# A hybrid decoder layer on one core: start addresses of split weights, and transposes in four visits instead of eight

## The chip, the cores and the metric

The kernel runs on one core of a Trainium2 chip. The metric is the device time of one execution in microseconds (us); below stands the median of several runs. One more execution was taken with the hardware profiler: the trace and the profile's page come from it.

## The reference

One layer over 256 tokens of 2048 features (batch 1), all in float32: two token mixers side by side (an mLSTM in chunks and an RWKV-7 scan), a cross-attention into 256 memory tokens, and a feed-forward part with a causal convolution and a GELU gate. Each part stands between two RMS norms and is added to the residual stream. Cut to what matters:

```python
h = rms_norm(x, mix_pre_norm)
proj = h @ w_in                                  # 2048 x 10536
ha = mlstm_chunkwise(q, k, v, i, f) ...          # 4 heads, chunks of 64 tokens
hb = rwkv7_scan(r, decay, k, v, kk, kk * a) ...  # 16 heads of 64
merged = sigmoid(g_a) * (ha @ w_branch_a) + sigmoid(g_b) * (hb @ w_branch_b)
x = x + rms_norm(merged @ w_mix_out, mix_post_norm)
x = x + rms_norm(cross_attention(rms_norm(x), rms_norm(mem), wq, wkv, wo), xattn_post_norm)
u = rms_norm(x, ffn_pre_norm) @ w_up             # 2048 x 16384
uc = conv_b + sum(conv_w[j] * shift_right(u, 2 - j) for j in range(3))
gate, up = split_cols(uc, (8192, 8192))
x = x + rms_norm((gelu(gate) * up) @ w_down, ffn_post_norm)
```

## The kernel before

**Products in split form.** A float32 product is made of three matmuls in the chip's faster 32-bit format (fp32r): each operand is split into a high part, rounded to that format, and the low rest. For activations these are pairs such as `hh`, `hl` or `fh`, `fl`; for weights `wh`, `wl`. A product is high x high, low x high and high x low. The file's helper `mm` records every matmul on line 181.

**Weight chunks.** All weights come in 648 chunks of 128 partitions x 1024 elements or fewer (512 KB), numbered 0 to 647 in the order of use. A transfer on SyncE's queue loads each into `raw`, ACT casts it to `wh` (line 401), VectorE subtracts to make `wl` (line 441), and TensorE uses both. Transfers run six chunks ahead, casts and subtractions up to three. `wh` and `wl` have four buffers each, taken in turn, so chunks with the same number modulo 4 share one.

**Two forms.** In an "fm" block (features on partitions) 128-column pieces of the weights are the stationary operand, loaded into the array by LDWEIGHTS, and 256 tokens of activations stream past as the moving operand. A chunk has two halves (k = 2 rows of 512 columns) and 24 matmuls. In a "tm" block (tokens on partitions) the activations are stationary and the weights move: 512 columns a matmul, or 296 in the small projection (`w_sm`, chunks 8 to 15, 12 matmuls a chunk). The block "xv" moves 256 columns.

**Order.** Chunks 0 to 7 are RWKV's first projection, 8 to 15 the small one, 16 to 103 the other RWKV and mLSTM projections, 104 to 199 the gates and branches, 200 to 231 the mixer's output, 232 to 263 the cross-attention (xk 232 to 239, xv 240, 241 and 250 to 255, xq 242 to 249, xo 256 to 263), 264 to 519 the up-projection (blocks fu0 and fu1 interleaved, then fu2 at 280 to 287, fu3 at 288 and so on) and 520 to 647 the down-projection (fd0, fd1).

**Side work.** Evacuation of blocks, norms, the scan and attention are generators that `Spread` runs a piece at a time between half chunks: `half()` advances a tick, so a chunk has two ticks. A generator added with `chain=n` has one piece every n ticks, the first after `phase` ticks. Pieces that need TensorE put their matmuls into the stream at that place. `x_tokens` is such a generator: it is started in the evacuation of fu0, transposes the residual stream (`xr`, features by tokens) into `xt` (tokens by features) through PSUM tiles `xt` of the pool `aux` (four banks), and ACT copies each tile out. `xt` is used at the very end of the kernel. The block fu2 holds two `aux` banks until its evacuation.

**Where a chunk lies in its buffer.** `staged` gives each `wh` and `wl` a view into a buffer of 1152 elements: it starts at element `o`, and its second half lies `e` elements behind the first. Usually `o` is 16 (64 bytes), and 0 for "tm" chunks of 512 columns and more. A chunk in the table `KICK` is shifted: kind 2 starts it 96 bytes in instead of 64, so that both halves are shifted; kind 0 does so too and puts the second half another 96 bytes on; kind 1 shifts only the second half, by 32 bytes.

Of the kernel before, what the change touches and what calls it, by code (L numbers as in the profile page):

```python
# [15 lines left out]
P = 128  # L16
# [123 lines left out]
def layer(tc, d, dbg=None):  # L140
    with ExitStack() as ctx:
        ctx.enter_context(tc.manual_schedule())
        _layer(ctx, tc, tc.nc, d, dbg or (lambda n, t: None))


def _layer(ctx, tc, nc, d, dbg):
    act, dve = Meter(nc.scalar, 200.0, 0.83), Meter(nc.vector, 70.0, 1.04)
    pool, pe, sp = nc.gpsimd, nc.tensor, nc.sync
    side = Spread(act, dve)
# [6 lines left out]
    def U(name, shape=None, dt=F32):  # L156
        return mp.tile(shape or [P, 8, S], dt, tag="U", bufs=7, name=name)
# [10 lines left out]
    def C(name, tag, shape=None, dt=F32):  # L168
        return mp.tile(shape or [P, S], dt, tag=tag, bufs=1, name=name)
# [7 lines left out]
    def aux(name, shape=None):  # L177
        return pp.tile(shape or [P, 512], F32, tag="aux", bufs=4, name=name)
# [63 lines left out]
    def bc(ap, n):  # L242
        return ap.unsqueeze(1).broadcast_to((ap.shape[0], n, ap.shape[1]))
# [94 lines left out]
    def block(kind, srcs, xs, evac, before=None, cols=512, pool_=None, pre=None, bankwise=False, tail=0):  # L338
# [2 lines left out]
                           pool=pool_ or acc, pre=pre, task=None, bankwise=bankwise, tail=tail))  # L341
        return blocks[-1]

    KICK = {16: 0, 18: 2, 36: 2, 52: 1, 60: 2, 104: 0, 108: 0, 111: 0, 116: 0, 117: 1, 120: 1, 134: 0, 138: 2, 140: 0, 159: 1,
            168: 0, 216: 2, 219: 2, 236: 2, 243: 2, 257: 2, 266: 2}

    HB = [slice(0, 256), slice(256, 512)]

    class Feed:
# [34 lines left out]
        def staged(self, name, r, i):  # L384


            k, c = r.shape[1:]
            kick = KICK.get(i)
            e = -(-c // 64) * 64
            o = 0 if c >= 512 and self.kind[i] == "tm" else 16  # L390
            if kick is not None:
                o, e = ((24, e + 24), (o, e + 8), (24, e))[kick]
            w = wp.tile([P, 1024 + 128], F32R, tag=name, bufs=4, name=name)
            return w[:, o:o + k * e].rearrange("p (k c) -> p k c", k=k)[:, :, 0:c]
# [1447 lines left out]
    def actile(k):  # L1842
        while len(M["ac"]) <= (k // 16 if k < 32 else 2 + (k - 32) // 8):
            n = len(M["ac"])
            M["ac"].append(big("ac") if n < 2 else U("ac"))
        return M["ac"][k // 16][:, k % 16] if k < 32 else M["ac"][2 + (k - 32) // 8][:, (k - 32) % 8]

    def fu_evac(b):
        def gen(ps):
            us = [C("us", f"bg{g}", [P, 2, S]) for g in range(2)]  # L1850
            tt = [[C("tg", f"m{j}") for j in range(2)], [C("tu", f"mt{j}") for j in range(2)]]
            cv = M["cv"]

            def base(i):
                for j in range(2):
                    f = i * 64 + b * 2 + j
                    act.activation(tt[i][j], us[i][:, j], AF.Identity, scale=cv[:, 2, f:f + 1], bias=cv[:, 3, f:f + 1])

            def taps(i):
                for j in range(2):  # L1860
                    f = i * 64 + b * 2 + j
                    o, u = tt[i][j], us[i][:, j]
                    dve.scalar_tensor_tensor(o[:, 1:S], u[:, 0:S - 1], cv[:, 1, f:f + 1], o[:, 1:S],
                                             op0=ALU.mult, op1=ALU.add)
                    dve.scalar_tensor_tensor(o[:, 2:S], u[:, 0:S - 2], cv[:, 0, f:f + 1], o[:, 2:S],
                                             op0=ALU.mult, op1=ALU.add)

            if b == 0:
                yield from M["res"].wait(30)
                side.add(x_tokens(), chain=8)  # L1870
            dve.tensor_mul(us[0], ps[0], bc(stf.rb, 2))
            yield
            base(0)
            dve.tensor_mul(us[1], ps[1], bc(stf.rb, 2))
            yield
            base(1)
            taps(0)
            yield
            for j in range(2):
                act.activation(tt[0][j], tt[0][j], AF.Gelu_apprx_tanh)  # L1880
            taps(1)
            yield
            for j in range(2):
                dve.tensor_mul(actile(b * 2 + j), tt[0][j], tt[1][j])
            yield
        return gen
# [49 lines left out]
    def x_tokens():  # L1936

        M["xt"] = []
        for f in range(4):
            if f % 2 == 0:  # L1940
                M["xt"].append(U("xt", [P, 2, 1024]))
            for t in range(2):
                q = aux("xt", [P, 4, P])
                for j in range(4):
                    k = f * 4 + j
                    pe.transpose(q[:, j], M["xr"][k // 8][:, k % 8, t * P:(t + 1) * P], ident)  # L1946
                act.copy(M["xt"][f // 2][:, t, f % 2 * 512:f % 2 * 512 + 512], q.rearrange("p a b -> p (a b)"))
                yield

    def load_gain():  # L1950
        M["gain"] = mp.tile([P, D], F32, tag="hT", bufs=2, name="gain")
# [175 lines left out]
```

## Time and profile before

| | us |
|---|---|
| median of 3 runs (1863.1 to 1864.75) | 1863.75 |
| the profiled execution's own time | 1862.86 |
| its span, first to last instruction | 1861.0 |
| TensorE busy | 1851.9 |
| VectorE busy | 1296.2 |
| ScalarE (ACT) busy | 1015.3 |
| transposes `xt`, first and last start | 856.8 and 936.5 |

The profiled execution is 1.86 us longer than its span; what lies around the span is the start and the end of the program. "PE" in the rows is TensorE's matmuls, "PEld" its weight loads, "DVE" is VectorE. Matmuls overlap in the array, so the length of a row is more than its share of the time: what counts is the distance from one start to the next. In rows of the time-ordered view the first number is the start in us from the span's start, the second the length, and xN the number of instructions merged into the row.

### The profile page before, as it was taken

The numbers are of one execution on the slowest core, as the hardware profiler recorded it, in microseconds if no ns is written. First come the engines' busy times: TensorE is split into PE (matmuls) and PEld (weight loads), VectorE is DVE, ScalarE is ACT, GpSimd is POOL, SyncE is SP. The second block draws the span as 40 slices with busy tenths as digits, with TensorE's granted clock in tenths as the row PEclk, the third lists the DMA queues.
The fourth block names the chain that finished last, engine by engine and source line by source line (L and its number), as shares of the span: only waits on it lengthen the run. The fifth ranks groups of instructions, "written<-read, shape, count | busy, mean of one in ns | idle before, by whom it ended". The sixth has DMA issues, their size and how long they took to land.

```text
span 1861.0 us, 36212 instructions
## 1 busy us (share of the span) xinstructions
PE 1851.9 (100%) x14930; PEld 1767.3 (95%) x14930; DVE 1296.2 (70%) x1834; ACT 1015.3 (55%) x1493; POOL 34.8 (2%) x64
## 2 busy tenths in 40 slices
PE   9999999999999999999999999999999999999998
PEld 9999888999999999999999999999999988888887
DVE  7889787566676858787766667766666775556555
ACT  6776445555454746666554455444445554545544
POOL 0100020000000000000000000000000000000000
PEclk9999999999999999999999999999999999999999
DMA  7556545455556765555666666666666666666664
GB/s 263 192 174 192 181 153 163 133 164 156 177 190 195 273 203 182 161 183 172 197 196 195 196 193 193 192 193 195 195 196 194 195 193 215 192 193 192 194 192 145
DMA packets 98486, 351.47 MB, mean 189 GB/s; under 512 B 10960, under 2 KB 11984, under 8 KB 97936
## 3 DMA queue, kind: packets, MB, share of 16 engines
q1 hardware_dynamic: 97744, 348.23, 59.8%
q8 instruction: 117, 1.92, 0.4%
q10 hardware_dynamic: 576, 0.92, 0.1%
q14 instruction: 49, 0.40, 0.1%
HBM read 347.01 MB, written 2.10 MB: 188 GB/s over the span
## 4 chain that ended last, share of the span: by engine, by line
PE 99%; DMA 0%; DVE 0%; ACT 0%; issue 0%; DVEq 0%; ACTq 0%
PE fm L181 69%; PE tm L181 25%; DMA w<-in_w_in_dram 0%; PE gram L181 0%; PE Y L181 0%; PE num L181 0%; PE lv L181 0%; PE X L181 0%; PE U L181 0%; PE zg L181 0%; PE zwa L181 0%; PE xsc L181 0%; PE xt L1946 0%; PE stb L181 0%; PE Tn L181 0%; PE xo L181 0%
## 5 line engine op out<-in xcount | busy, mean ns | idle before, releaser
L441 DVE TENSOR_TENSOR wl<-raw,wh 128x1024 fp32r<-128x1024 f32 (+1 forms) x639 | 774.9, 1218 | 415.3 <-ACT wh L401 407.6
L401 ACT CAST wh<-raw 128x1024 fp32r<-128x1024 f32 (+1 forms) x639 | 663.9, 1044 | 472.7 <-PE fm L181 358.7
L181 PE MATMUL fm<-fh,wh 128*128 128x256 f32 x2048 | 565.4, 277 | 0.6 <-DVE fh L66 0.6
L181 PE MATMUL fm<-fl,wh 128*128 128x256 f32 x2048 | 564.4, 277 | 0.0
L181 PE MATMUL fm<-fh,wl 128*128 128x256 f32 x2048 | 564.4, 277 | 0.0
L181 PEld LDWEIGHTS fm<-fh,wh 128*128 128x128 f32 x2048 | 383.9, 188 | 0.8 <-DVE fh L66 0.8
L181 PEld LDWEIGHTS fm<-fl,wh 128*128 128x128 f32 x2048 | 383.8, 188 | 0.0
L181 PEld LDWEIGHTS fm<-fh,wl 128*128 128x128 f32 x2048 | 383.7, 188 | 0.0
L181 PE MATMUL tm<-wh,as 128*128 128x512 f32 x1024 | 315.6, 390 | 0.0
L181 PE MATMUL fm<-hh,wh 128*128 128x256 f32 x1024 | 284.5, 280 | 0.7 <-ACT wh L401 0.6
L181 PE MATMUL fm<-hh,wl 128*128 128x256 f32 x1024 | 282.1, 277 | 0.8 <-DVE wl L441 0.8
L181 PE MATMUL fm<-hl,wh 128*128 128x256 f32 x1024 | 282.0, 277 | 0.0
L181 PEld LDWEIGHTS tm<-wh,as 128*128 128x128 f32 x1024 | 192.2, 188 | 39.9
L181 PE MATMUL tm<-wl,as 128*128 128x512 f32 x512 | 199.5, 390 | 0.0
L181 PEld LDWEIGHTS fm<-hh,wh 128*128 128x128 f32 x1024 | 192.2, 189 | 1.7 <-ACT wh L401 0.8
L181 PEld LDWEIGHTS fm<-hh,wl 128*128 128x128 f32 x1024 | 191.5, 188 | 1.0 <-DVE wl L441 1.0
L181 PEld LDWEIGHTS fm<-hl,wh 128*128 128x128 f32 x1024 | 191.7, 188 | 0.1
L181 PEld LDWEIGHTS tm<-wl,as 128*128 128x128 f32 x512 | 96.1, 188 | 19.9
L66 ACT CAST as<-ac 128x256 fp32r<-128x256 f32 x128 | 45.6, 404 | 110.8 <-PE tm L181 110.8
L66 DVE TENSOR_TENSOR as<-ac,as 128x256 fp32r<-128x256 f32 x128 | 48.6, 421 | 61.7 <-ACT as L66 61.7
L181 PE MATMUL fm<-mgh,wh 128*128 128x256 f32 x256 | 71.1, 278 | 0.0
L181 PE MATMUL fm<-mgl,wh 128*128 128x256 f32 x256 | 70.9, 277 | 0.0
(411 smaller groups left out, 2224.5 us busy)
## 6 DMA issues: line engine op xcount, KB each, us to landing
raw<-in_w_fu_dram SPq DMA_DIRECT2D x256, 512.0 KB, 4.3
raw<-in_w_in_dram SPq DMA_DIRECT2D x152, 512.0 KB, 3.5
raw<-in_w_fd_dram SPq DMA_DIRECT2D x128, 512.0 KB, 4.0
raw<-in_w_br_dram SPq DMA_DIRECT2D x32, 512.0 KB, 4.2
raw<-in_w_mo_dram SPq DMA_DIRECT2D x32, 512.0 KB, 3.8
raw<-in_w_xk_dram SPq DMA_DIRECT2D x8, 512.0 KB, 3.6
raw<-in_w_xv_dram SPq DMA_DIRECT2D x8, 512.0 KB, 3.6
raw<-in_w_xq_dram SPq DMA_DIRECT2D x8, 512.0 KB, 4.0
```

The costliest lines, as they stand in the source:

```text
L66: return f(out, *a, **k)
L181: pe.matmul(out, lhsT, rhs, start=start, stop=stop, skip_group_check=True)
L401: nc.scalar.copy(wh, r)
L441: nc.vector.tensor_sub(wl, r, self.st[self.nl][0])
```

## The change

Three edits of placement and order; every operation and its size stays.

```diff
-    KICK = {..., 134: 0, 138: 2, 140: 0, 159: 1,
-            168: 0, 216: 2, 219: 2, 236: 2, 243: 2, 257: 2, 266: 2}
+    KICK = {..., 134: 0, 137: 2, 140: 0, 159: 1,
+            168: 0, 215: 2, 219: 2, 235: 2, 242: 2, 257: 2, 266: 2, 282: 2}
...
         def staged(self, name, r, i):
...
-            o = 0 if c >= 512 and self.kind[i] == "tm" else 16
+            o = 0 if self.kind[i] == "tm" else 16
...
         def fu_evac(b):
...
             if b == 0:
                 yield from M["res"].wait(30)
-                side.add(x_tokens(), chain=8)
+                side.add(x_tokens(), chain=16, phase=24)
...
         def x_tokens():
...
-            for t in range(2):
-                q = aux("xt", [P, 4, P])
+            qs = [aux("xt", [P, 4, P]) for _ in range(2)]
+            for t, q in enumerate(qs):
                 for j in range(4):
                     k = f * 4 + j
                     pe.transpose(q[:, j], M["xr"][k // 8][:, k % 8, t * P:(t + 1) * P], ident)
+            for t, q in enumerate(qs):
                 act.copy(M["xt"][f // 2][:, t, f % 2 * 512:f % 2 * 512 + 512], q.rearrange("p a b -> p (a b)"))
-                yield
+            yield
```

The small projection's chunks (8 to 15, 296 columns) now start at byte 0 of their buffers instead of byte 64. The kicks of chunks 138, 216, 236 and 243 move to the chunk before, and chunk 282 gets one. These edits change addresses alone and leave the order of instructions as it was. The transposes were eight visits of four (token half t = 0 or 1), eight ticks apart, the first as soon as `x_tokens` is added; they become four visits of eight (both halves), sixteen ticks apart, the first after 24 ticks. On TensorE the second visit of before stands so among the matmuls of fu2:

```order
L181 MATMUL fm<-fl,wh 128x256
L181 MATMUL fm<-fh,wl 128x256
L1946 MATMUL xt<-con,xr_7843 128x128 x4
L181 MATMUL fm<-fh,wh 128x256
L181 MATMUL fm<-fl,wh 128x256
L181 MATMUL fm<-fh,wl 128x256
```

The first visit of the changed kernel stands at the start of chunk 295, in fu3 (`con` holds the identity):

```order
L181 MATMUL fm<-fl,wh 128x256
L181 MATMUL fm<-fh,wl 128x256
L1946 MATMUL xt<-con,xr_7843 128x128 x8
L181 MATMUL fm<-fh,wh 128x256
L181 MATMUL fm<-fl,wh 128x256
L181 MATMUL fm<-fh,wl 128x256
```

The old visits are at the starts of chunks 283, 287, 291, 295, 299, 303, 307 and 311, the new ones at 295, 303, 311 and 319. On ACT the copies move with them. Just behind the statistic `stf` of the difference stands:

```order
 L66 ACTIVATE stf_b<-stf_b 128x256
-L401 CAST wh<-raw 128x1024
-L66 COPY xt<-xt 128x512
-L401 CAST wh<-raw 128x1024
+L401 CAST wh<-raw 128x1024 x2
 L66 ACTIVATE tg<-us,cv 128x256 x2
 L66 ACTIVATE tu<-us,cv 128x256 x2
```

and at the new first visit, in the changed kernel alone:

```order
L66 ACTIVATE tg<-tg 128x256 x2
L401 CAST wh<-raw 128x1024 x3
L66 COPY xt<-xt 128x512 x2
L401 CAST wh<-raw 128x1024 x2
L66 ACTIVATE tg<-us,cv 128x256 x2
```

The two copies of a visit now follow each other, with three casts ahead of them and two behind.

More of the change, by code (lines that the diff above doesn't have):

```diff
@@ L342, in block @@
         return blocks[-1]
-    KICK = {16: 0, 18: 2, 36: 2, 52: 1, 60: 2, 104: 0, 108: 0, 111: 0, 116: 0, 117: 1, 120: 1, 134: 0, 138: 2, 140: 0, 159: 1,
-            168: 0, 216: 2, 219: 2, 236: 2, 243: 2, 257: 2, 266: 2}
+    KICK = {16: 0, 18: 2, 36: 2, 52: 1, 60: 2, 104: 0, 108: 0, 111: 0, 116: 0, 117: 1, 120: 1, 134: 0, 137: 2, 140: 0, 159: 1,
+            168: 0, 215: 2, 219: 2, 235: 2, 242: 2, 257: 2, 266: 2, 282: 2}
     HB = [slice(0, 256), slice(256, 512)]
```

## The prediction

> **What bounds the kernel now.** I read the page from the top (busy shares, then the chain that ended last), then busy time by windows, then the time-ordered rows of the tensor engine around every place that the change touches.
>
> ```profile
> span 1861.0 us, 36212 instructions
> PE 1851.9 (100%) x14930; PEld 1767.3 (95%) x14930; DVE 1296.2 (70%) x1834; ACT 1015.3 (55%) x1493; POOL 34.8 (2%) x64
> ...
> PE 99%; DMA 0%; DVE 0%; ACT 0%; issue 0%; DVEq 0%; ACTq 0%
> ```
>
> TensorE is busy for 1851.9 of 1861.0 us and 99% of the chain of work is on it: no copy, cast or transfer decides anything, and a change can only show in how fast matmuls start one after the other. So I look at start-to-start times, not at busy shares. In the windows view (stretch, its length, busy time and matmuls in it) the long up-projection and the down-projection run so:
>
> ```profile
> 950.00:1500.00 550.00, 550.00 (x4855) 1.00 0.65 195
> 1520.00:1670.00 150.00, 150.00 (x664) 1.00 0.66 202
> ```
>
> Less the two or so begun before each stretch, a 256-column matmul takes 550/4853 = 113.3 ns and a 512-column one 150/662 = 226.6 ns, twice as much. 24 matmuls of 113.3 ns make 2.72 us for one weight chunk ("fm", 256 columns). Whatever a chunk takes beyond 2.72 is what this change can win or lose.
>
> **The slow pace.** The next rows (start, length) are chunks 281 to 283 and one later visit of the transposes.
>
> ```profile
> 852.15 0.59 PE L181 MATMUL stb<-stf,ones 128*128 128x256 f32 x2
> 852.39 0.47 PE L181 MATMUL fm<-fh,wh 128*128 128x256 f32 x1
> ...
> 854.00 0.28 PE L181 MATMUL fm<-fh,wh 128*128 128x256 f32 x1
> ...
> 856.70 0.28 PE L181 MATMUL fm<-fh,wl 128*128 128x256 f32 x1
> 856.83 0.60 PE L1946 MATMUL xt<-con,xr 128*128 128x128 f32 x4
> 857.18 0.37 PE L181 MATMUL fm<-fh,wh 128*128 128x256 f32 x1
> ...
> 868.04 0.28 PE L181 MATMUL fm<-fh,wl 128*128 128x256 f32 x1
> 868.16 0.60 PE L1946 MATMUL xt<-con,xr 128*128 128x128 f32 x4
> 868.52 0.37 PE L181 MATMUL fm<-fh,wh 128*128 128x256 f32 x1
> 868.73 0.28 PE L181 MATMUL fm<-fl,wh 128*128 128x256 f32 x1
> ...
> 879.50 0.60 PE L1946 MATMUL xt<-con,xr 128*128 128x128 f32 x4
> ```
>
> Behind the two "stb" matmuls of a statistic, chunk 282 (854.00 to 856.70, 23 steps) runs at 117.6 ns a matmul, 4.3 above the steady pace, with nothing waited for. The first visit of the transposes (856.83) ends that: from 868.73 to 879.50 lie 95 matmuls of four chunks at 113.4. So an interruption by other matmuls can leave TensorE in a slow pace, 0.10 us a chunk, or take it out of it. What the kick table does (it shifts where a chunk's two halves lie) shows in chunk 18, kicked out of the fast pace, and in chunk 236, kicked out of the slow one:
>
> ```profile
> 48.78 0.28 PE L181 MATMUL fm<-hh,wh 128*128 128x256 f32 x1
> 51.67 0.28 PE L181 MATMUL fm<-hh,wh 128*128 128x256 f32 x1
> ...
> 712.50 0.47 PE L181 MATMUL fm<-mh,wh 128*128 128x256 f32 x1
> 714.11 0.28 PE L181 MATMUL fm<-mh,wh 128*128 128x256 f32 x1
> 716.92 0.28 PE L181 MATMUL fm<-mh,wh 128*128 128x256 f32 x1
> 719.64 0.28 PE L181 MATMUL fm<-mh,wh 128*128 128x256 f32 x1
> ```
>
> Chunk 18 takes 2.89 us (120 ns a matmul), a pure loss of 0.17. Chunk 236 (714.11 to 716.92) takes 2.81, and chunk 237 is back at 2.72. A kick is thus a price of 0.09 (from slow) to 0.17 us (from fast), paid once to end a state that costs 0.10 a chunk.
>
> **The change, part by part.** *The transposes (8 visits of 4 become 4 of 8).* The 32 transposes stay; four entries and exits go. One visit of four costs 868.73 - 868.16 = 0.57, less the 0.11 of the one matmul among it: 0.46 us. Eight in a row exist already, the "vt" transposes ahead of the kicked chunk 60:
>
> ```profile
> 171.39 1.03 PE L1057 MATMUL vt<-con,vT 128*128 128x128 f32 x8
> 172.18 0.36 PE L181 MATMUL fm<-hh,wh 128*128 128x256 f32 x1
> 172.38 0.28 PE L181 MATMUL fm<-hl,wh 128*128 128x256 f32 x1
> ...
> 175.12 0.29 PE L181 MATMUL fm<-hh,wh 128*128 128x256 f32 x1
> ...
> 177.85 0.28 PE L181 MATMUL fm<-hh,wh 128*128 128x256 f32 x1
> ```
>
> 172.38 - 171.39 - 0.11 = 0.88 us. Against 2 x 0.46 that saves 0.04 a pair, at the rows' rounding 0.02 to 0.05; for four pairs -0.1 us (bounds -0.2 and 0, if the pace behind is the fast one; the slow one is a rival). The order of the program puts the new visits at the starts of chunks 295, 303, 311 and 319, where fu2's evacuation is over, so that the two PSUM banks that a visit now takes at once are free; the copies out of them follow as pairs on ACT, 2 x 0.6 us:
>
> ```profile
> L66 ACT COPY xt<-xt x8: 566/588/588, 857.5 to 936.8; 128x512 f32<-128x512 f32 x8
> ```
>
> Casts run two to three chunks (5.4 to 8.2 us) ahead of their matmuls and ACT is busy 55%, so that costs nothing; with that lead gone it would be the 0.6 us of the second copy, four times. No DMA and no DVE instruction moves.
>
> *The moved kicks.* Rows where each now stands behind the interruption:
>
> ```profile
> 428.22 0.39 PE L181 MATMUL fm<-hh,wh 128*128 128x256 f32 x1
> 433.98 0.28 PE L181 MATMUL fm<-hh,wh 128*128 128x256 f32 x1
> ...
> 655.62 0.36 PE L181 MATMUL fm<-mgh,wh 128*128 128x256 f32 x1
> 661.35 0.28 PE L181 MATMUL fm<-mgh,wh 128*128 128x256 f32 x1
> ...
> 730.52 0.28 PE L181 MATMUL fm<-qh,wh 128*128 128x256 f32 x1
> 736.17 0.28 PE L181 MATMUL fm<-qh,wh 128*128 128x256 f32 x1
> ```
>
> Chunks 137+138 take 5.76, 215+216 5.73, 242+243 5.65: one slow chunk and one kicked out of it. With the kick in the first, the nearest row is chunk 60, kicked right behind an interruption, with its neighbour: 177.85 - 172.18 = 5.67, and 5.58 without its long first matmul (0.09), which 242 has not. That gives -0.09, -0.06 and -0.07, of which I take 0.02 back for 137, whose first matmul is longer: -0.20 together. Chunk 235 is interrupted in its middle (712.50): its kick now costs its fast first half 12 x 7 ns = 0.08 and its second half about what 236's half costs, and saves the 0.09 of 236 and the 0.05 of the slow half: -0.01, nothing. The new kick of 282 makes a chunk of 117.6 ns one like 236 (117.1): -0.01. Sum of the kicks -0.2 us; bounds -0.4 (each pair down to a kicked chunk of 2.81 and a steady one, with its long first matmul kept) and +0.1 (each kicked at chunk 18's 120 ns, and 235 for its whole length).
>
> *The small projection.* Its eight chunks have 12 matmuls of 296 columns each.
>
> ```profile
> 28.83 0.30 PE L181 MATMUL tm<-wh,hh 128*128 128x296 f32 x1
> ...
> 30.43 0.29 PE L181 MATMUL tm<-wh,hh 128*128 128x296 f32 x1
> ...
> 725.08 0.28 PE L181 MATMUL tm<-wh,mh 128*128 128x256 f32 x1
> ```
>
> 1.60/12 = 133.3 ns; in proportion to the two windows 296 columns would take 131.0. All that an aligned start could bring is 96 x 2.3 ns = 0.22 us. The 512-column chunks that keep the proportion do start at a chunk's first byte, but the two chunks 240 and 241, whose 256 moving columns start 64 bytes in, run from 725.08 to 730.52 (above) at 5.44/48 = 113.3 ns as well. The first speaks for the whole 0.22, the second for nothing; I take half, -0.1; bounds -0.3 (all at the shortest spacing of 130 ns) and +0.2 (all at the longest, 135).
>
> Here the Trainium skill speaks against: "SBUF — State Buffer", Specifications, gives lines of 16 bytes, and 0, 64 and 96 bytes are all starts of such lines, so neither a kick nor this move could do anything. The trace disagrees with that for kicks (2.89 and 2.81 against 2.72 us); for the small projection no run here shows it yet. By the page the sum would be the -0.1 of the transposes alone.
>
> Sum: -0.1 - 0.2 - 0.1 = -0.4 us on the profiled execution's 1862.86 us. The median of the runs shown, 1863.75, is 0.9 above that execution; taking the same off gives 1863.3. The bounds add up to -0.9 and +0.3. The runs shown spread by 1.65 us (1863.1 to 1864.75), so under 0.2% (3.7 us) no single measurement of this kernel can tell a difference from none.
>
> **Rivals.** *Slower: eight transposes leave the slow pace.* All other places with eight of them have a kick in or right behind them, so the trace has no unkicked outcome, and chunk 60 at (175.12 - 172.38)/23 = 119 ns lies between a chunk kicked out of slow and one out of fast. New visits have no kick behind them. If the last one, at 319, ends slow, nothing interrupts TensorE until the down-projection: 201 chunks x 0.10 = +20 us, 1884. It decides from 37 slow chunks on (3.7/0.10), which only the last visit can leave. Against it: transposes keep one spacing, 0.43 us for the second four in "vt" as for four alone in 868.16 to 868.52 with entry, so the end of a visit does not know how many came before; the last four of each new visit are those of every second old visit, as at 868.16, at chunk starts of the same ring buffer; that one came out fast (113.4 above), and so did the last, as the window from 950 shows. Chance 8%.
>
> The Trainium skill would rule this rival out: "TensorE: Matmul & The Clock Gate", Step-by-step: what each phase is for, says that weight loads and moving columns have read ports of their own, so that loading ahead takes nothing from a running matmul. The slow 117.6 ns with no wait is against a pace so free of the other stream, whatever its cause.
>
> *A moved kick fails.* If the one at 282 does not end the slow pace, it lasts the 12 chunks to the first visit, which are 12 x 0.10 = +1.2; 242 failing costs some eight chunks, +0.8; 235 seven, +0.7. Time 1864 to 1866, still inside 0.2%. For it: a kick right behind an interruption meets another state than one a chunk later. Against: 236 came out fast, and 60, kicked at once, within a few matmuls (177.85 - 175.12 = 2.73). Chance 12%.
>
> *Nothing comes through:* alignment of 64 bytes means nothing for moving columns and early kicks cost what late ones did: -0.1, 1863.6. Chance 20%.
>
> *Faster than forecast:* no mechanism; all visits together cost 8 x 0.46 = 3.7 us and the transposes themselves stay. 2%.
>
> **How the numbers follow.** The forecast with its bounds has 58%, nothing 20%, a failed kick 12%, the slow pace 8%, faster 2%. All but the last two stay within 0.2%: same 0.90, slower 0.08, faster 0.02. The range 1861.9 to 1865.6 takes the bounds (1862.9 to 1864.0), about 1 us below and above for how the median of a few runs scatters, and most of a failed kick; it leaves out the slow pace.
>
> **What would show it.** Right: four "xt" rows of x8 at chunks 295, 303, 311 and 319, about 0.79 us to the next matmul and 113.3 ns behind each; chunk pairs from 137, 215 and 242 near 5.67, 5.65 and 5.58; the small projection's 12 starts in under 1.60 us. Wrong: any long stretch at 117.6 ns, above all from 960 on, or a small projection still at 133.3.

## The result: slower, 1888.4 against 1864.3 us

The changed kernel takes 1888.41 us (median of 4 runs, 1888.07 to 1889.18), the kernel before 1864.25 us beside it (4 runs, 1863.1 to 1864.89). The ratio is 1.0131, with a 95% interval of 1.0113 to 1.0148. My forecast was 1863.3 us; what came is the rival "eight transposes leave the slow pace", to which I gave 8% and 1884 us.

The page of the changed kernel, span and busy times:

```profile
span 1886.4 us, 36215 instructions
PE 1877.1 (100%) x14930; PEld 1792.6 (95%) x14930; DVE 1296.6 (69%) x1834; ACT 1018.6 (54%) x1493; POOL 34.8 (2%) x64
```

The span grew by 25.4 us and TensorE's busy time by 25.2, with the same 14930 matmuls; VectorE and ACT change little (+0.4 and +3.3 us). No wait of TensorE grew by more than 0.3 us; the matmuls themselves follow each other more slowly. The windows view, in a stretch of the up-projection and one of the down-projection (stretch, its length, then busy time and number of instructions of PE, PEld, DVE, ACT and POOL, the granted clock, and two columns on transfers):

```profile
975.00:1525.00 550.00, 550.00 (x4672) 550.00 (x4672) 365.01 (x486) 267.42 (x343) 0.00 (x0) 1.00 0.62 187
1535.00:1685.00 150.00, 150.00 (x664) 124.20 (x663) 91.33 (x119) 76.38 (x114) 0.00 (x0) 1.00 0.66 200
```

In 550 us of the up-projection now stand 4672 matmuls and not 4855: 550/4670 = 117.8 ns each, the slow pace of the prediction, while the granted clock (the 1.00) is the same. The down-projection is untouched: 664 matmuls as before. The visits of the transposes in the time-ordered view, first at chunk 295, second at 303, last at 319:

```profile
891.00 1.04 PE L1946 MATMUL xt<-con,xr 128*128 128x128 f32 x8
891.79 0.36 PE L181 MATMUL fm<-fh,wh 128*128 128x256 f32 x1
891.99 0.28 PE L181 MATMUL fm<-fl,wh 128*128 128x256 f32 x1
...
914.49 1.03 PE L1946 MATMUL xt<-con,xr 128*128 128x128 f32 x8
...
961.47 1.04 PE L1946 MATMUL xt<-con,xr 128*128 128x128 f32 x8
962.26 0.36 PE L181 MATMUL fm<-fh,wh 128*128 128x256 f32 x1
962.47 0.28 PE L181 MATMUL fm<-fl,wh 128*128 128x256 f32 x1
```

A visit takes the 0.79 us that I forecast. But from 891.99 to 914.49 the 191 matmuls take 117.8 ns each; the same holds between the later visits, and behind the last one to the end of the up-projection. The groups of weight loads in the slow stretch (three rows of the changed kernel) and in the steady one (one row of the kernel before, whose other two also read 188); behind the number of loads stand their busy time in us, the mean length of one in ns, and the idle time in front of them:

```profile
L181 PEld LDWEIGHTS fm<-fh,wh 128*128 128x128 f32 x1557 | 298.9, 192 | 0.0
L181 PEld LDWEIGHTS fm<-fh,wl 128*128 128x128 f32 x1558 | 292.5, 188 | 0.0
L181 PEld LDWEIGHTS fm<-fl,wh 128*128 128x128 f32 x1557 | 292.3, 188 | 0.0
```

```profile
L181 PEld LDWEIGHTS fm<-fh,wh 128*128 128x128 f32 x1618 | 303.9, 188 | 0.0
```

In the slow pace the records of one load in three are 4 ns longer, with no wait in front of any (last column).

Where the 25.4 us came from, by the start-to-start times of the chunks in the two traces (an interruption ahead of a chunk counts to that chunk):

| stretch | us |
|---|---|
| chunks 0 to 7, first arrival of the weights | +0.2 |
| small projection, 8 to 15 | +0.23 |
| 16 to 103 | +0.06 |
| kicks 137 and 215 (137 to 217) | +0.15 - 0.02 - 0.05 |
| kicks 235 and 242 (235 to 249) | +0.65 + 0.47 |
| 250 to 281, no part of the change | -0.14 |
| 282 to 294: kick 282, three old visits gone | -1.39 |
| 295 to 319: new visits, slow pace | +3.88 |
| 320 to 519: slow pace, 200 x 0.107 | +21.34 |

The first row is no effect of the change: between executions those eight chunks differ by 0.2 to 2.2 us in the traces of this study. Single times therefore tell effects of 20 us, and the traces tell those of a tenth.

The moved kicks (chunks 137 to 139; 215 to 217; 236, 237, 242, 243, 244 and 249; 282 to 284), first matmul of each:

```profile
428.71 0.39 PE L181 MATMUL fm<-hh,wh 128*128 128x256 f32 x1
431.67 0.28 PE L181 MATMUL fm<-hh,wh 128*128 128x256 f32 x1
434.50 0.28 PE L181 MATMUL fm<-hh,wh 128*128 128x256 f32 x1
...
656.24 0.37 PE L181 MATMUL fm<-mgh,wh 128*128 128x256 f32 x1
659.17 0.29 PE L181 MATMUL fm<-mgh,wh 128*128 128x256 f32 x1
661.91 0.28 PE L181 MATMUL fm<-mgh,wh 128*128 128x256 f32 x1
...
714.78 0.28 PE L181 MATMUL fm<-mh,wh 128*128 128x256 f32 x1
717.60 0.28 PE L181 MATMUL fm<-mh,wh 128*128 128x256 f32 x1
...
731.74 0.28 PE L181 MATMUL fm<-qh,wh 128*128 128x256 f32 x1
734.59 0.28 PE L181 MATMUL fm<-qh,wh 128*128 128x256 f32 x1
737.42 0.28 PE L181 MATMUL fm<-qh,wh 128*128 128x256 f32 x1
...
751.55 0.28 PE L181 MATMUL fm<-qh,wh 128*128 128x256 f32 x1
...
855.54 0.28 PE L181 MATMUL fm<-fh,wh 128*128 128x256 f32 x1
858.36 0.28 PE L181 MATMUL fm<-fh,wh 128*128 128x256 f32 x1
861.08 0.28 PE L181 MATMUL fm<-fh,wh 128*128 128x256 f32 x1
```

Chunk 138 still takes 2.83 us: the kick of 137 did not end the slow pace. Chunks 215 and 216 take 5.67 together, against 5.73 before: that kick worked. Behind the kick of 235, chunks 237 to 241 take (731.74 - 717.60)/5 = 2.83 each; behind that of 242, chunks 243 to 248 take (751.55 - 734.59)/6 = 2.83: both failed. Chunk 282 takes 2.82 and 283 is back at 2.72: that kick worked.

And the first chunk of the small projection, first matmul of chunks 8 and 9:

```profile
29.02 0.30 PE L181 MATMUL tm<-wh,hh 128*128 128x296 f32 x1
...
30.66 0.30 PE L181 MATMUL tm<-wh,hh 128*128 128x296 f32 x1
```

1.64 us for 12 matmuls, 1.60 before.

### The profile page after: what moved, and what is told of

Its sections match the earlier page's. It is cut to its first block, busy times and chain, and to the rows that moved or that the text cites. A ratio compares the mean times of both kernels' runs of the same rounds, so it can differ in the third digit from the quotient of the medians.

```text
span 1886.4 us, 36215 instructions
## 1 busy us (share of the span) xinstructions
PE 1877.1 (100%) x14930; PEld 1792.6 (95%) x14930; DVE 1296.6 (69%) x1834; ACT 1018.6 (54%) x1493; POOL 34.8 (2%) x64
## 4 chain that ended last, share of the span: by engine, by line
PE 99%; DMA 0%; DVE 0%; ACT 0%; issue 0%; DVEq 0%; ACTq 0%
PE fm L181 69%; PE tm L181 25%; DMA w<-in_w_in_dram 0%; PE gram L181 0%; PE Y L181 0%; PE num L181 0%; PE lv L181 0%; PE X L181 0%; PE U L181 0%; PE zg L181 0%; PE zwa L181 0%; PE xsc L181 0%; PE xt L1946 0%; PE stb L181 0%; PE Tn L181 0%; PE xo L181 0%
## 5 line engine op out<-in xcount | busy, mean ns | idle before, releaser
L181 PE MATMUL fm<-fh,wh 128*128 128x256 f32 x2048 | 572.9, 281 | 0.6 <-DVE fh L66 0.6
L181 PE MATMUL fm<-fh,wl 128*128 128x256 f32 x2048 | 572.2, 280 | 0.0
L181 PE MATMUL fm<-fl,wh 128*128 128x256 f32 x2048 | 572.2, 280 | 0.0
L181 PEld LDWEIGHTS fm<-fh,wh 128*128 128x128 f32 x2048 | 390.7, 191 | 0.8 <-DVE fh L66 0.8
```

The costliest lines, as they stand in the source:

```text
L181: pe.matmul(out, lhsT, rhs, start=start, stop=stop, skip_group_check=True)
```

## The experiments

In what follows a visit "meets" the pace of the matmuls ahead of it and "leaves" the pace of those behind it: a visit that leaves the slow pace has slow matmuls behind it.

**The visits alone.** The kernel before with the changed `x_tokens` and `side.add(x_tokens(), chain=16, phase=24)`; table of kicks and small projection as before.

> The kernel before with the four visits of eight transposes alone; kicks and small projection as before. Theory (eight transposes leave TensorE at the slow pace, 117.8 ns a matmul instead of 113.3): without the kick at 282 the slow pace also fills chunks 282 to 294, so nearly the whole loss and a little more is here: +24 to +26 us, about 1889, all of it in the up-projection from chunk 282 to 519. Rival (the moved kicks are what makes the slow pace, the visits are innocent): within 2 us of before, 1864 to 1866, with a fast pace behind chunk 319.

1889.37 us (1888.94 to 1889.98) against 1864.05, ratio 1.0136 (1.012 to 1.0151). The windows view:

```profile
975.00:1525.00 550.00, 550.00 (x4672) 550.00 (x4672) 365.05 (x486) 267.49 (x341) 0.00 (x0) 1.00 0.61 187
```

The same 4672 matmuls. The visits carry the loss, without any kick being moved. Chunk 282, not kicked here and with no visit at 283, stayed slow until 295, so the first visit met a slow pace and did not end it either.

**The kicks alone.** The kernel before with the changed table.

```diff
-            KICK = {..., 138: 2, ..., 216: 2, 219: 2, 236: 2, 243: 2, ..., 266: 2}
+            KICK = {..., 137: 2, ..., 215: 2, 219: 2, 235: 2, 242: 2, ..., 266: 2, 282: 2}
```

> The kernel before with the changed kick table alone. Theory: chunks 137, 235 and 242, kicked right behind an interruption or in it, stay slow as in the changed kernel (138, 139; 236 to 241; 243 to 249), 215 and 282 come out fast: +1.2 to +1.6 us, 1865 to 1866. Rival (the kicks carry the loss): +25 us, 1889.

1865.59 us (1864.86 to 1866.95) against 1864.05, ratio 1.0008 (0.9999 to 1.0017). By chunk it repeats the changed kernel: 137 to 140 +0.15 us, 215 to 217 -0.05, 235 to 241 +0.65, 242 to 249 +0.47, so +1.2 us where I forecast -0.2. In all six traces of this study with the moved table, 137, 235 and 242 failed and 215 worked; in all eight with the old one, the kicks of 138, 216, 236 and 243 worked. So the outcome at a place repeats from execution to execution. In this trace chunks 283 to 286 also run at 117.8 ns, until the visit at 287, though 283 is steady in the other five. That need not be a failed kick: this run alone keeps the old visit of four at 283, right behind the kicked chunk, and it does not tell the two apart.

**A kick behind each visit.** The changed kernel with a kick one chunk behind every visit of eight.

```diff
-            ..., 266: 2, 282: 2}
+            ..., 266: 2, 282: 2, 296: 2, 304: 2, 312: 2, 320: 2}
```

> The changed kernel with one more kick of kind 2 in the chunk after each visit (296, 304, 312, 320). Theory (the loss is a state that any kick a chunk after the interruption ends): each visit costs one slow chunk, one kicked chunk, then 113.3 ns again; the 24.2 us shrink to about 1 to 2: 1865 to 1866.5. Rival (the slow pace comes from something that lasts, such as the changed rhythm of copies on ACT or the addresses of the transposed tiles): the pace returns to 117.8 ns after each kick, 1886 or more.

1867.05 us (1866.09 to 1869.23), ratio to the kernel before 1.0018 (1.0008 to 1.0028): 21.4 us of the loss are back, with all four visits of eight in place. The windows view (like those of some runs below, this stretch ends in the down-projection, whose matmuls are twice as long):

```profile
975.00:1525.00 550.00, 550.00 (x4782) 547.17 (x4782) 380.78 (x511) 277.09 (x360) 0.00 (x0) 1.00 0.64 194
```

So what cost the time is the pace behind a visit, and not the visit. The ten runs fall into two groups, 1866.1 to 1866.3 and 1867.9 to 1869.2; the trace is of the first, and what differed in the second was not seen. The way there was not smooth: the kick of 296 ended the slow pace, that of 304 did not, and the visits at 311 and 319 left the steady pace by themselves, so that the kicks of 312 and 320 cost 0.16 us each for nothing.

**One visit taken apart, the last.** The changed kernel, whose last visit becomes two of four, eight chunks apart.

```diff
                     pe.transpose(q[:, j], M["xr"][k // 8][:, k % 8, t * P:(t + 1) * P], ident)
+                if f == 3 and t == 0:
+                    yield
```

> The changed kernel, its last visit alone split into two visits of four (at chunk 319 and at 327). Theory (a visit of eight leaves the slow pace, a visit of four from the slow pace ends it, as all eight did in the kernel before): slow at about 117.8 ns from 295 to 319, then 113.3 ns behind 319 or at the latest behind 327, so about 200 x 0.107 = 21.4 us under the changed kernel: near 1867. Rival (the place or the buffers of chunks 295 to 319, or the two banks, hold the slow pace, not the number in a row): slow to chunk 519 all the same, near 1888.

1867.78 us, once. Slow from 295 on as in the changed kernel, and steady right behind the visit of four at 319:

```profile
975.00:1525.00 550.00, 550.00 (x4790) 547.44 (x4789) 381.17 (x514) 278.10 (x363) 0.00 (x0) 1.00 0.63 194
```

The count is not quite comparable with the 4855 of before, since this stretch ends in 15 us of the down-projection, whose matmuls are twice as long: 535/0.1133 + 15/0.2266 = 4788. Against the 1888.4 us of the changed kernel, whether the last eight stand in a row or not is worth 20.6 us.

**One visit put together, the last.** The reverse: the kernel before, whose last two visits become one of eight at chunk 307.

```diff
+            qs = []
             for t in range(2):
-                q = aux("xt", [P, 4, P])
+                qs.append(aux("xt", [P, 4, P]))
                 ...
-                act.copy(...)
-                yield
+                if f < 3:
+                    act.copy(...)
+                    yield
+        for t, q in enumerate(qs):
+            act.copy(...)
```

> The kernel before with its last two visits of four made one of eight (at chunk 307); the six ahead stay at four, and kicks and small projection stay as they were. Theory (one visit of eight out of the steady pace leaves the slow pace in most cases, five of seven so far as first visit behind a steady stretch): slow from 307 to 519, 213 chunks x 0.107 = 22.8 us, near 1887. Rival (the slow pace comes from the row of four visits of eight, or from the place 295): 113.3 ns behind 307, near 1864.

1886.41 us, once; expected were 1887. The slow pace runs from 307 to 519:

```profile
975.00:1525.00 550.00, 550.00 (x4673) 550.00 (x4671) 365.31 (x487) 268.39 (x343) 0.00 (x0) 1.00 0.61 187
```

One visit of eight out of the steady pace is enough, at another chunk than the change has. With the run above, it shows the cause from both sides.

**Half a chunk later.** The changed kernel with `phase=25`, so each visit stands between the two halves of its chunk.

> The changed kernel, each visit of eight one tick later: in the middle of chunks 295, 303, 311 and 319 and not at their start. Theory (eight in a row leave the slow pace wherever they stand): slow from the middle of 295 to 519, 1888. Rival (what decides is where in a chunk TensorE is interrupted, so which buffer is being read): fast behind some of the visits, the last with them, near 1867.

1889.28 us, once, and 4672 matmuls again in the stretch from 975 to 1525. So the loss does not need a visit at the start of a chunk.

**Eight within one chunk, not in a row.** The changed kernel, the two groups of four twelve matmuls apart (`yield` behind the first group, and fourteen idle ticks behind the second).

> The changed kernel, its four visits of eight each taken apart into four and four with twelve matmuls of 256 columns between them (first half of chunks 295, 303, 311 and 319). Theory (eight in a row set the slow pace, four leave the steady one or end the slow one): 113.3 ns behind all of them, near 1867. Rival (eight transposes within a chunk do it, in a row or not): 117.8 ns to chunk 519, near 1888.

1865.89 us, once; behind each of the eight groups of four the steady pace follows:

```profile
975.00:1525.00 550.00, 550.00 (x4781) 547.13 (x4780) 380.76 (x511) 277.31 (x361) 0.00 (x0) 1.00 0.64 194
```

So eight in a row do it, not eight in a chunk: with twelve matmuls of 256 columns between four and four the slow pace does not come.

**The number in a row.** Four more experiments put visits of unused transposes into the long steady stretch behind chunk 319, in the kernel before:

```diff
+        side.add(probe(), chain=1, free=True)      # at the end of x_tokens
+    def probe():
+        for gap, n, banks, mode in PROBE:
+            for _ in range(gap):
+                yield
+            qs = [aux("lad", [P, 4, P]) for _ in range(banks)]
+            for i in range(n):
+                ...
+                pe.transpose(q[:, i % 4], src, ident)   # mode "mm": mm(q[:, i % 4], src, ident)
```

First a ladder: n = 4, 8, 1, 2, 3, 5, 6, 7, 9, 10, 11, 12, 14, 16, 8, eight chunks apart, each with a kick of kind 2 four chunks behind.

> The kernel before with its own eight visits of four, and then fifteen more visits, 16 ticks apart from chunk 327 on, which transpose tiles of xt into PSUM for nobody: 4, 8, 1, 2, 3, 5, 6, 7, 9, 10, 11, 12, 14, 16 and 8 transposes, with a kick of kind 2 four chunks behind each so that the next one starts at the fast pace. What is read is the pace of the three chunks behind each visit. Theory A (the length of the visit, taken modulo something short, sets how weight loads and matmuls lie to one another): 4 fast, 8 slow, and others scattered over 1 to 16, with 8 slow both times. Theory B (long visits leave the slow pace): fast up to some number between 4 and 8, slow for all above. Theory C (the operands or the place, not the number): 4 and 8 alike.

Four of its windows, 8 us each, behind visits of 3, 6, 7 and 11 (73 matmuls are the steady pace, 70 or 71 the slow one):

```profile
1074.18:1082.18 8.00, 8.00 (x73) 8.00 (x73) 6.45 (x11) 5.65 (x9) 0.00 (x0) 1.00 0.48 162
1118.96:1126.96 8.00, 8.00 (x73) 8.00 (x73) 6.17 (x10) 5.62 (x9) 0.00 (x0) 1.00 0.50 165
1141.58:1149.58 8.00, 8.00 (x70) 8.00 (x70) 5.97 (x10) 5.38 (x9) 0.00 (x0) 1.00 0.51 166
1211.28:1219.28 8.00, 8.00 (x73) 8.00 (x72) 5.61 (x9) 5.06 (x9) 0.00 (x0) 1.00 0.52 167
```

Out of the steady pace, visits of 3, 4, 5 and 6 left it steady, 7, 8, 9, 10, 12 and 16 slow, 11 and 14 steady. Out of the slow pace, 1 left it slow, 2 ended it, and the second visit of 8 ended it too. No theory of a clean bound or of a period fits all of that: up to six is harmless here, above that it is mostly not. Three of the kicks failed (more on that below).

Then the same number many times: eight visits of eight and eight of four, every 8.5 chunks, each with a kick five chunks behind.

> The kernel before with sixteen more visits of unused transposes in the long run at the steady pace, every 8.5 chunks from chunk 327 on, so at starts and middles of chunks in turn: eight visits of eight, then eight of four, each with a kick of kind 2 five chunks behind it. Theory (the number in a row decides): slow behind all eight of eight, fast behind all eight of four. Rival (the outcome hangs on the moment, and the number only shifts the moment): a mixture in both groups.

The first four visits of eight and the first of four, 10 us behind each (91 is steady, 88 slow):

```profile
982.68:992.68 10.00, 10.00 (x88) 10.00 (x87) 7.79 (x13) 5.75 (x9) 0.00 (x0) 1.00 0.54 154
1007.31:1017.31 10.00, 10.00 (x88) 10.00 (x87) 8.32 (x14) 6.40 (x10) 0.00 (x0) 1.00 0.53 158
1032.21:1042.21 10.00, 10.00 (x91) 10.00 (x90) 9.25 (x15) 5.38 (x9) 0.00 (x0) 1.00 0.53 164
1056.40:1066.40 10.00, 10.00 (x91) 10.00 (x90) 7.98 (x14) 5.76 (x8) 0.00 (x0) 1.00 0.52 165
...
1178.77:1188.77 10.00, 10.00 (x91) 10.00 (x90) 4.78 (x4) 3.24 (x4) 0.00 (x0) 1.00 0.70 205
```

Of eight: slow, slow, steady, steady, slow, steady, steady, slow, at starts and middles of chunks alike. Of four: eight times steady. So my theory held for four and was too strong for eight.

Over all 14 traces, counting the visits `xt` and the added ones (those with a kick in the interrupted chunk itself left out): of transposes in visits of four, all 71 that met the steady pace left it steady, and 10 of 11 that met the slow one ended it; the exception stands right behind the kicked chunk 282 of the kicks alone. Of 24 visits of eight that met the steady pace, 19 left the slow one. The five others have something in common: the visit ahead of each met a slow pace, which is so for none of the 19. And of 17 visits of eight that met a slow pace, the 12 with no kick since the visit before left it slow, and the five with a kick that had failed in between ended it. So for visits of eight something besides the pace decides, and the traces do not show what it is.

**What the interrupting matmuls are.** Eleven visits, eight chunks apart, kick four chunks behind: transposes into two banks or one, of eight slices or one, and plain float32 matmuls (each shown as two records).

> The kernel before with eleven more visits, eight chunks apart from chunk 327, whose results are unused, each followed by a kick of kind 2 four chunks behind: 8 transposes into two banks; 8 into one; 8 of one source slice into two banks, and into one; 4 of one slice; 4 plain float32 matmuls of 128 columns; 8 of them into two banks, and into one; 2; 1; and 8 transposes again. Theory (the length of the interruption sets where TensorE's loads come to stand against its matmuls): plain matmuls of the same length act as transposes do, four fast and eight mostly slow; banks and source do not matter. Rival one (two PSUM banks at once do it): eight into one bank fast. Rival two (the moving operand's addresses do it): eight of one slice fast.

Eight transposes into one bank left the slow pace out of the steady one (chunk 335), so the two banks are not it. Eight of one slice into one bank left it steady, and eight of one slice into two ended a slow one; but both stand where the state above also had them steady, so whether addresses count is open. Plain matmuls behind which 8 us were counted, first eight of them (1.70 us long), then one (0.14 us):

```profile
1144.04:1152.04 8.00, 8.00 (x73) 8.00 (x72) 5.04 (x9) 4.49 (x8) 0.00 (x0) 1.00 0.49 163
1190.17:1198.17 8.00, 8.00 (x71) 8.00 (x70) 6.49 (x11) 5.76 (x9) 0.00 (x0) 1.00 0.53 163
```

Eight (tried twice), four (0.81 us) and two of them left the steady pace, one left the slow one. So neither is a long interruption bad in itself nor a short one good: four plain matmuls take nearly as long as eight transposes (0.81 and 0.79 us) and came out the other way. My theory of the length fell in the form in which I had it, that about the same length gives the same pace; whether the 0.02 us between the two matter, no run shows.

**Kicks behind a visit of eight.** Ten visits of eight, kicked with kinds 0, 1 and 2 at distances of 0 to 2 chunks.

> The kernel before with ten more visits of eight unused transposes, eight chunks apart from chunk 327, each followed by a kick: kind 2 at a distance of 0, 1 and 2 chunks, kind 0 at 0 and 1, kind 1 at 0 and 1, none, kind 2 at 0 and 1; and a kick of kind 2 five chunks behind each visit. Theory (a kick in the interrupted chunk itself meets the transition and not a settled slow pace, and so fails more often): distance 0 leaves the slow pace in most cases, distance 1 and 2 end it. Rival (a kick ends the slow pace by chance, wherever it stands): as many failures at 1 and 2 as at 0.

Two of its places, kind 2 one chunk behind a visit (chunks 336 to 338), and kind 0 in the interrupted chunk (351 to 353):

```profile
1009.80 0.28 PE L181 MATMUL fm<-fh,wh 128*128 128x256 f32 x1
1012.61 0.28 PE L181 MATMUL fm<-fh,wh 128*128 128x256 f32 x1
1015.44 0.28 PE L181 MATMUL fm<-fh,wh 128*128 128x256 f32 x1
...
1053.27 0.37 PE L181 MATMUL fm<-fh,wh 128*128 128x256 f32 x1
1056.17 0.28 PE L181 MATMUL fm<-fh,wh 128*128 128x256 f32 x1
1058.89 0.28 PE L181 MATMUL fm<-fh,wh 128*128 128x256 f32 x1
```

Kind 2 one chunk behind failed (2.81, then 2.83 us), two chunks behind it worked, and in the interrupted chunk it worked once and failed once. Kinds 0 and 1 worked in all four tries. Over the added kicks of kind 2 that met a settled slow pace, in this and the other experiments, 12 ended it and 10 did not. The theory that distance decides is not borne out, and the rival of chance is not needed: the traces tell the two groups apart. In the settled slow pace one of the three loads of a product takes 192 ns, and it is not always the same one. Ahead of the failed kick of chunk 336 and of the one of chunk 340, which worked, it is (chunks 335 and 339; the other loads read 188):

```profile
L181 PEld LDWEIGHTS fm<-fh,wl 128*128 128x128 f32 x8 | 1.5, 192 | 0.0
L181 PEld LDWEIGHTS fm<-fh,wh 128*128 128x128 f32 x8 | 1.5, 192 | 0.0
```

All ten kicks that failed met the slow pace with the load of high x low (`fh`, `wl`) long, and behind each of them the load of high x high is long. All twelve that worked met it with high x high (5) or low x high (7) long. So it is with all 66 kicks of kind 2 of the old table that met a settled slow pace in the 14 traces: none met the long load at high x low, and each ended the pace. This is read out of runs made for something else, and no run was set up to test it. For visits of eight the long load alone does not decide: of ten that met it at high x high, the five behind a failed kick ended the slow pace, the five others did not.

**The small projection alone.** The kernel before with `o = 0 if self.kind[i] == "tm" else 16` as its one edit.

> The kernel before with the small projection's start at byte 0 as the one edit. Theory (the start at byte 0 slows these eight chunks): 135.8 ns a matmul in chunks 8 to 15 as in the changed kernel, against 133.3, so +0.2 us, seen in the trace alone. Rival (the start-up noise of one execution did it): 133.3 ns as before. Either way one time cannot tell it: 1863 to 1866.

1863.88 us, once, where single times tell nothing of this size. Chunk 8 to chunk 9:

```profile
29.08 0.30 PE L181 MATMUL tm<-wh,hh 128*128 128x296 f32 x1
...
30.72 0.30 PE L181 MATMUL tm<-wh,hh 128*128 128x296 f32 x1
```

1.64 us as in the changed kernel; over the eight chunks the edit adds 0.23 us, in every trace that has it, and in none that has not. By the Trainium skill, "SBUF — State Buffer", Specifications, bytes 0 and 64 both start a line of 16 bytes, so the move should do nothing; the run disagrees, by 2.4 ns (0.23 us over 96 matmuls) in 133.3 for a matmul of 296 columns.

## Why the prediction was wrong

**The step that failed** is in the rival that I kept small: "the end of a visit does not know how many came before". I took the outcome of four for that of eight, because the last four of a new visit are those of an old one and stand at the same chunk starts. The runs with the last visit taken apart and put together show the reverse: eight in a row in place of four cost 20.6 us at 319 and 22.9 us at 307 (1886.41 against 1863.56 us, a single run beside it). The durations on which I argued were right (0.79 us to the next matmul; 109 ns from one transpose to the next in four as in eight, though the text sets 0.43 us beside a stretch of 0.36); the pace behind a visit does not follow from them. That all other places with eight transposes had a kick behind them, which I named, was the better evidence, and at 8% I gave it too little. (One place had none: eight transposes of 4x4, `gcol`, ahead of chunk 28, with 113.3 ns a few matmuls later; of another shape, they stand for neither side.)

**The price of that rival** was right in its terms: 201 chunks by 0.107 us are 21.5, 20 in the text, which takes 0.10 a chunk. It lacked the three visits ahead of the last: the pace was slow from 295 on, another 24 x 0.107 = 2.6 us. And the "Against" in it rested on the one step above; no second reason from the rows stood behind the 8%.

**The moved kicks** were forecast at -0.2 and came out at +1.2 us. Two terms were right: 215 and its neighbour at 5.67 as forecast, and 282. The others failed, as the rival "a moved kick fails" has it: 235 cost +0.65 where the text has +0.7, 242 +0.47 where it has +0.8. There six chunks stayed slow and not eight, 0.64 us, and the step from the last of their matmuls to the next statistic, 0.32 us before, took 0.12 us, which gave 0.2 us back. What failed as a step is the use of chunk 60 as the row for "a kick right behind an interruption works": 215 bears it out, 137 does not, and why these two differ stays open.

**The small projection** was forecast at -0.1 and is +0.23, with the sign wrong and just outside its bounds (-0.3 to +0.2). The 512-column chunks that start at byte 0 were no row for one of 296 columns.

**The transposes' own time** was right: entry and exit of a visit of eight against two of four save some hundredths of a us. ACT's paired copies cost nothing, as forecast: TensorE's matmul groups show no idle time that grew.

**The Trainium skill's rule** that I set against the rival, in "TensorE: Matmul & The Clock Gate", Step-by-step: what each phase is for, that loads ahead take nothing from a running matmul, did not rule the slow pace out: it is there, at 117.8 ns a matmul over 550 us, with one load in three at 192 and not 188 ns. Whether the loads are what slows the matmuls, no run here shows.

**A better kernel** was not found. What the matmuls of 256 columns in the kernel before take beyond 113.3 ns, the two steps at each interruption left out, adds up to 4.0 us over chunks 16 to 519, and the kicks that look like pure loss are not: that of 257 met a slow pace in four of the 14 traces, that of 266 in two.

## What to carry to other kernels

Where the same stream of matmuls can run at two paces without any wait, an edit that interrupts it has two prices: its own time, and the pace that it leaves times the work up to the next interruption; the second was here 24 times the first (21.4 us behind the last visit, 0.9 us for it), so look first at what follows the last interruption. Keep interruptions in the form that the trace shows to be harmless (here four transposes, with other matmuls in between), and count an outcome seen at one place as one sample. A correction tuned to one place, such as a shifted start address, is not to be moved by one chunk on the strength of another that worked.

## What was not expected of the hardware

- A stream of 256-column matmuls has a steady pace of 113.3 ns and a slow one of 117.8 ns at the same granted clock of 1.00, and holds either for 200 chunks (560 us) if nothing interrupts it.
- Eight transposes in a row (0.79 us) out of the steady pace left the slow one in 19 of 24 cases, four (0.36 us) in none of 71; plain float32 matmuls of 0.81 (tried once) and 1.70 us (twice) did not, one of 0.14 us (once) did.
- The same visit of eight comes out differently behind another history; what is remembered stays open.
- In the slow pace one load in three takes 192 and not 188 ns. Starting one chunk's weights 32 bytes later (kind 2) ended the pace in all 12 added cases where the long load was that of high x high or low x high, and in none of 10 where it was that of high x low.
- For weights of 296 columns as the moving operand a start at byte 0 is slower than at byte 64: about 135.8 against 133.3 ns a matmul.
